# A two-layer RWKV/S5 trunk on one core: state-space tables made in whole-tensor operations, low-rank weights scaled once, and squares summed on TensorE in the last norm

## The chip, the cores and the metric

The kernel runs on one core of a Trainium2 chip. The metric is the device time of one execution in microseconds (us); lower is better. PE is TensorE, DVE VectorE, ACT ScalarE, POOL GpSimd, SP SyncE (its queue issues all DMAs of this kernel).

## The reference, cut to what matters

1024 tokens of width 1024 go through two layers in float32, each a token mixer and a squared-ReLU MLP, each followed by a LayerNorm of `alpha*x + f(x)`. What the change touches:

```
xw = x + xx * mu[1]; xa = x + xx * mu[4]; xg = x + xx * mu[5]   # xx: the token before, minus x
tanh(xw @ w1);  xa @ a1;  sigmoid(xg @ g1)                       # low-rank factors of RWKV
abar = exp(dt * lam); bbar = coef * b                            # S5, complex, 64 groups x 64 states x 16 channels
layer_norm(alpha * h + mlp(h))                                   # the last of the four norms
```

## The kernel before, in words

All activations lie transposed, 128 channels on the partitions, as eight tiles of 512 tokens for each half H of the sequence. A float32 product is three matmuls: weight and operand are split into a rounded part and the rest (`split`: an ACT cast, L151, and a DVE subtraction, L152), and `mm3` adds hi*hi, hi*lo and lo*hi; all of these are on L203. Weights come in tiles of 128x512 (256 KB) through `wraw` (2 buffers), `whi` and `wlo` (3 each). Where both halves need the same weight, the first writes the rest `wlo` to DRAM (L183) and the second loads it (L177).

- **Low-rank factors** (`rwkv_proj`, once for each half). `x + xx*mu` times a weight W is `x @ ((1-mu)W)` plus the shifted `x @ (mu W)`. `scaled` loads W, lets POOL multiply it by `1-mu` or `mu` (L330), splits it and multiplies. `shifted` calls it twice for `wa1` and twice for `g1a`; `gate_c` calls it once, with both scalings side by side. That is ten weight tiles for each half.
- **Tables of S5** (`s5_tables`, rank 99500, run beside the first half's MLP, the second half's output projection and its first norm). L1080 to L1090 make the powers 0 to 8 of 32 complex numbers on each partition, one power after the other, six DVE operations each. For each of eight f, `bc` is loaded (L1129), `bb` made in six small DVE operations (L1135 to L1140), and `ca` and `bp` expanded: two products on POOL (L1152, L1155), two on DVE (L1153, L1156), and a sum each (L1154, L1157); `ca` also gets a change of sign (L1159). Then `ca` goes to DRAM (tC, L1163), PE multiplies it with `bb` (L1170), transposes `bp` (L1186), and the results go out through `kpad` (L1179, eight DMAs of 64 KB) and `bs` (L1188). `ca`, `bp`, `bc`, `bs` have one buffer each.
- **Last norm** (`last_norm`, in two parts c of 256 tokens). TensorE makes the mean (L929), DVE subtracts it from eight tiles (L932), ACT squares them (L934, L937), six additions on DVE and POOL (L938) leave two sums, which four matmuls turn into column sums (L942). Then comes the power on POOL (L945), a spread and transposes (L947, L950), the product (L952), scale and bias (L956 on ACT, one tile on POOL), and the store.

The order on each engine and queue is static. A planner simulates the program and issues, on each engine, the ready instruction of lowest rank; the waits at run time are semaphores, and every engine and queue runs strictly in that order. MLP work has rank 200000 and more, the norms 99000, so tables come before the MLP and after a norm.

Of the kernel before, what the change touches and what calls it, by code (L numbers as in the profile page):

```python
# [8 lines left out]
F32 = mybir.dt.float32  # L9
# [49 lines left out]
MIX0R = 1500  # L59
EVB = 4  # L60
# [11 lines left out]
def trunk(ctx, tc, A):  # L72
# [120 lines left out]
    def inorder(prods):  # L193

        for x, y in zip(prods, prods[1:]):
            tc.add_manual_dep(y.ins, x.ins.name, mybir.DependencyInfo(
                mybir.DependencyClass.NoSync, mybir.DependencyReason.DATA), reason="order")

# [43 lines left out]
    def psd():  # L242
        return pd.tile([128, HT], F32, tag="d", name="d")
# [9 lines left out]
    for j in range(2):  # L253
        V.tensor_copy(pick[:, j].rearrange("p (q n) -> p q n", q=4),
                      ident[:, 64 * j : 64 * j + 32].unsqueeze(1).broadcast_to([128, 4, 32]))

    def rwkv_proj(H):
# [65 lines left out]
        def scaled(nm, parts):  # L323
            p = psd()
            n = 128 // len(parts)
            for k0 in range(0, KT, 4):
                w = first.pop(0) if first else wraw(nm, k0)
                for q, m in enumerate(parts):
                    wq = w[:, :, q * n : q * n + n]
                    G.tensor_mul(wq, wq, m[:, k0 : k0 + 4].unsqueeze(2).broadcast_to([128, 4, n]))  # L330
                hi = wp.tile([128, 4, 128], F32R, tag="whi", name="whi")
                lo = wp.tile([128, 4, 128], F32R, tag="wlo", name="wlo")
                split(w, hi, lo)
                for k in range(4):
                    mm3(p, hi[:, k], lo[:, k], xo[k0 + k][0], xo[k0 + k][1], k0 + k == 0, k0 + k == KT - 1)
            return p

        def shifted(nm, ci, js):
            p1 = scaled(nm, [mum[:, j] for j in js])
            p2 = scaled(nm, [pv[:, j] for j in js])  # L340
            e = tp.tile([128, HT], F32, tag="ev", name="e2", bufs=EVB)
            S.copy(e, p2)
            hd = tp.tile([128, HT], F32, tag="ev", name="hd", bufs=EVB)
            V.tensor_add(hd[:, 1:], p1[:, 1:], e[:, 0 : HT - 1])
            if H == 0:
                V.tensor_copy(hd[:, 0:1], p1[:, 0:1])
                V.tensor_copy(carry_p[:, ci : ci + 1], e[:, HT - 1 :])
            else:
                V.tensor_add(hd[:, 0:1], p1[:, 0:1], carry_p[:, ci : ci + 1])
            return hd  # L350
# [563 lines left out]
    def last_norm(h, gi, c):  # L914
# [15 lines left out]
        sab = tp.tile([128, 2, HW], F32, tag="la", name="sq01", bufs=2)  # L930
        for k, t in enumerate(hc):
            V.tensor_sub(t, t, pm)  # L932
            if k < 2:
                S.activation(sab[:, k], t, AF.Square)  # L934
            else:
                q = tp.tile([128, HT], F32, tag="m", name="sq")[:, 0:HW]
                S.activation(q, t, AF.Square)  # L937
                (G if k in LNT else V).tensor_add(sab[:, int(k in LNT)], sab[:, int(k in LNT)], q)  # L938
        pq = pl.tile([128, HT], F32, tag="l", name="pq")
        for t in range(2):  # L940
            for j in range(2):
                PE.matmul(pq[:, t : t + 1], sab[:, j, t * 128 : (t + 1) * 128], ones_c[:, 0:1], start=j == 0, stop=j == 1)  # L942
# [100 lines left out]
    def s5_tables():  # L1043
# [6 lines left out]
        pw = pp.tile([128, 9, 2, 32], F32, name="pw")  # L1050
# [29 lines left out]
        V.memset(pw[:, 0, 0], 1.0)  # L1080
        V.memset(pw[:, 0, 1], 0.0)
        V.tensor_mul(pw[:, 1, 0], mg, tr)
        V.tensor_mul(pw[:, 1, 1], mg, tq)
        for j in range(2, 9):
            V.tensor_mul(pw[:, j, 0], pw[:, j - 1, 0], pw[:, 1, 0])
            V.tensor_mul(sn, pw[:, j - 1, 1], pw[:, 1, 1])
            V.tensor_sub(pw[:, j, 0], pw[:, j, 0], sn)
            V.tensor_mul(pw[:, j, 1], pw[:, j - 1, 0], pw[:, 1, 1])
            V.tensor_mul(sn, pw[:, j - 1, 1], pw[:, 1, 0])
            V.tensor_add(pw[:, j, 1], pw[:, j, 1], sn)  # L1090
        for l in range(4):
            re, im = aw[:, l, :, 0], bw[:, l, :, 1]
            if l == 0:
                V.tensor_copy(re, pw[:, 8, 0])
                V.tensor_copy(im, pw[:, 8, 1])
# [15 lines left out]
        V.tensor_scalar(nr, pw[:, 1, 0], -1.0, None, op0=ALU.add)  # L1111
        ni = pw[:, 1, 1]
# [10 lines left out]
        for kpad in kpads:  # L1123
            G.memset(kpad[:, :, 0:8], 0.0)
        for f in range(KT):
            gs = slice(4 * f, 4 * f + 4)
            kpad = kpads[f % 2]
            bc = pp.tile([128, 2, 2, 4, 16], F32, tag="bc", name="bc", bufs=1)
            SP.dma_start(bc, A["s5bc"][f])  # L1129
            bb = pp.tile([128, 2, 4, 16], F32, tag="bb", name="bb", bufs=1)  # L1130
            tw = pp.tile([128, 4, 9, 16], F32, tag="tw", name="tw", bufs=1)
            w3 = tw[:, :, 0]
            sh = [128, 4, 16]
            crb, cib = cr[:, gs].unsqueeze(2).broadcast_to(sh), ci[:, gs].unsqueeze(2).broadcast_to(sh)
            V.tensor_mul(bb[:, 0], bc[:, 0, 0], crb)  # L1135
# [9 lines left out]
            def expand(out, src, npow, neg):  # L1145
                sh4 = [128, 4, npow, 16]
                pr_ = pw[:, 0:npow, 0, gs].rearrange("p j g -> p g j").unsqueeze(3).broadcast_to(sh4)
                pi_ = pw[:, 0:npow, 1, gs].rearrange("p j g -> p g j").unsqueeze(3).broadcast_to(sh4)
                sr = src[0].unsqueeze(2).broadcast_to(sh4)
                si = src[1].unsqueeze(2).broadcast_to(sh4)  # L1150
                w = tw[:, :, 0:npow]
                G.tensor_mul(out[0], pr_, sr)  # L1152
                V.tensor_mul(w, pi_, si)  # L1153
                V.tensor_sub(out[0], out[0], w)  # L1154
                G.tensor_mul(out[1], pr_, si)  # L1155
                V.tensor_mul(w, pi_, sr)  # L1156
                V.tensor_add(out[1], out[1], w)  # L1157
                if neg:
                    V.tensor_scalar(out[1], out[1], -1.0, None, op0=ALU.mult)  # L1159

            expand((ca[:, :, 0], ca[:, :, 1]), (bc[:, 1, 0], bc[:, 1, 1]), 9, True)
            expand((bp[:, :, 0], bp[:, :, 1]), (bb[:, 0], bb[:, 1]), 8, False)
# [194 lines left out]
def layout(inp):  # L1357
# [46 lines left out]
    out["s5bc"] = bc.reshape(2, 2, 128, KT, 4, 16).transpose(3, 2, 0, 1, 4, 5)  # L1404
# [17 lines left out]
```

## Time and profile before

| | us |
|---|---|
| median of 3 runs | 2694.06 (2689.92 to 2696.62) |
| the profiled execution | 2690.84 |
| its span, first to last instruction | 2689.1 |
| PE / DVE / ACT / POOL busy | 2523.7 / 1818.4 / 1147.1 / 618.4 |

The span is the sum that the views divide up; 1.7 us lie around it. Busy PE counts pipelined matmuls, so it is not PE at its peak. DVE instructions overlap by some 0.08 us, so that sums of busy times of groups are a little over the engine's own.

### The profile page before, as it was taken

To read this page: it belongs to the slowest core of one execution; us is meant where nothing else is said; L and a number is where in the kernel's file an instruction comes from. 1 tells how busy PE (TensorE), PEld (TensorE's weight loads), DVE (VectorE), ACT (ScalarE), POOL (GpSimd) and SP (SyncE) were. 2 spreads that over 40 slices of the span, in tenths; PEclk is the share of its full clock that TensorE was granted. 3 is DMA by queue.
4 is the path that set the end of the run, shared out by engine and by line. 5 is a ranking of instruction groups with operands and counts; after the bars stand their busy time and mean duration, and the time that the engine had idled before them with its cause. 6 is when DMAs were issued, how large, how long until landed. Compare 5 with 4: busy or idle time off the path is not lost.

```text
span 2689.1 us, 44215 instructions
## 1 busy us (share of the span) xinstructions
PE 2523.7 (94%) x16768; PEld 2040.7 (76%) x16768; DVE 1818.4 (68%) x3206; ACT 1147.1 (43%) x2038; POOL 618.4 (23%) x516
## 2 busy tenths in 40 slices
PE   7999979999889999999998999999989999999997
PEld 5778757788677777667876788778778887788886
DVE  7367677487896868997677553675955536855556
ACT  7555665454444333234533332445233324533334
POOL 3121552342442122342121000121210001200001
PEclk9998989998889999999999999999999999999998
DMA  4765555663322224465335432223353322333333
GB/s 150 254 206 179 162 170 169 206 184 119 96 74 91 95 91 148 134 162 150 110 114 180 134 98 96 86 90 124 95 193 99 98 95 85 122 100 94 96 96 102
DMA packets 221972, 345.92 MB, mean 129 GB/s; under 512 B 21952, under 2 KB 84544, under 8 KB 221760
## 3 DMA queue, kind: packets, MB, share of 16 engines
q1 hardware_dynamic: 221760, 343.11, 40.5%
q8 instruction: 132, 2.16, 0.3%
q14 instruction: 80, 0.66, 0.1%
HBM read 279.06 MB, written 63.96 MB: 128 GB/s over the span
## 4 chain that ended last, share of the span: by engine, by line
PE 64%; DVE 16%; DMA 9%; issue 4%; ACT 4%; POOL 2%; SPq 1%; ACTq 0%; DVEq 0%; POOLq 0%
PE d L203 56%; DVE wlo L152 3%; DMA s_y<-yg 2%; DMA wraw<-in_mw_dram 2%; DMA yl<-s_y 1%; DVE hA L1008 1%; DVE oAl L152 1%; PE pA L612 1%; ACT whi L151 1%; DMA wraw<-in_wr_dram 1%; DMA wraw<-in_wv_dram 1%; DVE hB L1008 1%; DVE qbuf L152 1%; DVE t L1238 1%; PE pbu L1226 1%
## 5 line engine op out<-in xcount | busy, mean ns | idle before, releaser
L151 ACT CAST whi<-wraw 128x512 fp32r<-128x512 f32 x668 | 413.9, 620 | 945.9 <-PE d L203 610.9
L152 DVE TENSOR_TENSOR wlo<-wraw,whi 128x512 fp32r<-128x512 f32 x668 | 501.8, 752 | 401.6 <-ACT whi L151 397.4
L203 PE MATMUL d<-qbuf,whi 128*128 128x512 f32 (+1 forms) x2112 | 656.3, 393 | 32.8 <-DVE hA L1008 15.3
L203 PEld LDWEIGHTS d<-qbuf,whi 128*128 128x128 f32 x2112 | 390.7, 191 | 130.1 <-DVE hA L1008 21.7
L203 PE MATMUL d<-qbuf,wlo 128*128 128x512 f32 (+1 forms) x1056 | 410.4, 391 | 9.2 <-DVE wlo L152 9.1
L203 PE MATMUL d<-oAh,whi 128*128 128x512 f32 (+1 forms) x960 | 385.5, 408 | 12.2 <-ACT ev L433 7.6
L992 POOL TENSOR_TENSOR rl<-rl 128x512 f32<-128x512 f32 x128 | 144.8, 1131 | 1079.8 <-ACT rl L991 1079.6
L203 PE MATMUL d<-oAl,whi 128*128 128x512 f32 (+1 forms) x960 | 381.8, 401 | 8.4 <-DVE oAl L152 8.4
L203 PE MATMUL d<-oAh,wlo 128*128 128x512 f32 (+1 forms) x960 | 382.2, 403 | 1.6 <-DMA wlo<-low 1.6
L203 PE MATMUL d<-oBh,whi 128*128 128x512 f32 x704 | 279.1, 396 | 0.0
L203 PE MATMUL d<-oBh,wlo 128*128 128x512 f32 x704 | 277.6, 395 | 1.5 <-DVE wlo L152 1.5
L203 PE MATMUL d<-oBl,whi 128*128 128x512 f32 x704 | 276.1, 392 | 0.0
L203 PEld LDWEIGHTS d<-qbuf,wlo 128*128 128x128 f32 x1056 | 201.2, 191 | 54.7 <-DVE wlo L152 13.2
L203 PEld LDWEIGHTS d<-oAh,whi 128*128 128x128 f32 (+1 forms) x960 | 183.3, 193 | 55.6 <-ACT ev L433 9.7
L203 PEld LDWEIGHTS d<-oAl,whi 128*128 128x128 f32 (+1 forms) x960 | 183.5, 193 | 47.4 <-DVE oAl L152 10.7
L203 PEld LDWEIGHTS d<-oAh,wlo 128*128 128x128 f32 (+1 forms) x960 | 183.4, 192 | 41.6 <-DMA wlo<-low 1.8
L1008 DVE TENSOR_TENSOR hB<-hB,d 128x512 f32<-128x512 f32 (+1 forms) x256 | 164.2, 650 | 60.9 <-PE d L203 58.2
L1008 DVE TENSOR_TENSOR hA<-hA,d 128x512 f32<-128x512 f32 x240 | 161.9, 682 | 53.6 <-PE d L203 51.6
L203 PEld LDWEIGHTS d<-oBh,wlo 128*128 128x128 f32 x704 | 132.6, 188 | 33.2 <-DVE wlo L152 2.1
L203 PEld LDWEIGHTS d<-oBl,whi 128*128 128x128 f32 x704 | 132.6, 188 | 29.0 <-issue 0.5
L203 PEld LDWEIGHTS d<-oBh,whi 128*128 128x128 f32 x704 | 132.6, 188 | 28.7 <-issue 1.3
L152 DVE TENSOR_TENSOR qbuf<-rl,qbuf 128x512 fp32r<-128x512 f32 x128 | 97.2, 759 | 67.7 <-ACT qbuf L151 67.3
(370 smaller groups left out, 3702.6 us busy)
## 6 DMA issues: line engine op xcount, KB each, us to landing
wraw<-in_mw_dram SPq DMA_DIRECT2D x520, 256.0 KB, 2.6
wraw<-in_glu_dram SPq DMA_DIRECT2D x64, 256.0 KB, 2.6
low<-wlo SPq DMA_DIRECT2D x52, 256.0 KB, 2.9
wlo<-low SPq DMA_DIRECT2D x52, 256.0 KB, 3.7
wraw<-in_wk_dram SPq DMA_DIRECT2D x32, 256.0 KB, 3.3
wraw<-in_wr_dram SPq DMA_DIRECT2D x32, 256.0 KB, 3.9
wraw<-in_wv_dram SPq DMA_DIRECT2D x32, 256.0 KB, 4.3
yl<-s_y SPq DMA_DIRECT2D x32, 256.0 KB, 3.1
```

The lines of the kernel that those rows point to most:

```text
L151: S.copy(hi, src)
L152: (e or V).tensor_sub(lo, src, hi.bitcast(F32))
L203: bulk.append((PE.matmul(p, w, x, **kw).ins, x.shape[-1]))
L612: prods.append(PE.matmul(pp[h][:, cc, i], D.KB[j][hs, u].rearrange("p j l -> p (j l)"), D.AR[j][hs, u].rearrange("p j l -> p (j l)"), star ...
L992: G.tensor_mul(r, r, r)
L1008: V.tensor_add(z, z, p)
L1226: PE.matmul(p[qs, g2, ri], tb[:, g2, ri, qs], u[:, 2 * g2 + par], start=True, stop=True)
L1238: e.tensor_mul(t2[:, :, ri], x[:, :, 1 - ri], bw[:, l, g0:g1, ri : ri + 1].broadcast_to([128, g1 - g0, n]))
```

## The change

1. The powers are made by doubling (1; 2; 3 and 4; 5 to 8), four DVE operations for each step, in a layout with the power innermost. `bc` is loaded whole in four DMAs, and `bb` made for all f in four DVE operations; ACT makes negated and swapped copies (`b2`, `c2`, the sign of `c1`). The expansion has no POOL operation, no change of sign, copies power 0 on ACT, and takes four DVE products and one DVE sum of both parts, for `ca` (512 and 1024 elements) and for `bp` (448 and 896).
2. `shifted` splits W unscaled and multiplies; then POOL scales the same tile by mu in place, and it is split again. The result is p(W) - p(mu W) + shifted p(mu W). The scaled pairs are written to DRAM in the first half (12 DMAs of 256 KB) and loaded in the second, without POOL, cast or subtraction. `gate_c` does the same with W and mu W side by side.
3. In the second part of the last norm TensorE adds up all eight squared tiles (16 matmuls of one column), and two tiles get scale and bias on DVE (`LNV`).

```
+    V.tensor_sub(pick[:, 0], pick[:, 0], pick[:, 1])
...
+        def scaled(nm, k0, w, parts):
+            ws = pair()
+            if (nm, k0) in low:
+                for x, kept in zip(ws, low[nm, k0]):
+                    SP.dma_start(flat(x), kept)
+                return ws
...
+                if m is not None:
+                    wq = w[:, :, q * n : q * n + n]
+                    G.tensor_mul(wq, wq, m[:, k0 : k0 + 4].unsqueeze(2).broadcast_to([128, 4, n]))
+            split(w, *ws)
...
+            for x, kept in zip(ws, low[nm, k0]):
+                SP.dma_start(kept, flat(x))
+            return ws
...
+        def shifted(nm, ci, js):
+            p1, p2 = psd(), psd()
             for k0 in range(0, KT, 4):
                 w = first.pop(0) if first else wraw(nm, k0)
+                ws = pair()
+                split(w, *ws)
+                lowmm(p1, ws, k0)
+                lowmm(p2, scaled(nm, k0, w, [pv[:, j] for j in js]), k0)
             e = tp.tile([128, HT], F32, tag="ev", name="e2", bufs=EVB)
             S.copy(e, p2)
             hd = tp.tile([128, HT], F32, tag="ev", name="hd", bufs=EVB)
-            V.tensor_add(hd[:, 1:], p1[:, 1:], e[:, 0 : HT - 1])
+            V.tensor_sub(hd, p1, e)
+            V.tensor_add(hd[:, 1:], hd[:, 1:], e[:, 0 : HT - 1])
...
+            for k0 in range(0, KT, 4):
+                w = None if ("g1c", k0) in low else wraw("g1c", k0)
+                lowmm(p, scaled("g1c", k0, w, [None, pv[:, 5]]), k0)
...
+        if c == 1:
+            sq = [tp.tile([128, 2, HW], F32, tag="ev", name="sq2", bufs=EVB) for _ in range(4)]
+            for k, t in enumerate(hc):
+                V.tensor_sub(t, t, pm)
+                S.activation(sq[k // 2][:, k % 2], t, AF.Square)
+            pq = pl.tile([128, HT], F32, tag="l", name="pq")
+            for k in range(KT):
+                for t in range(2):
+                    PE.matmul(pq[:, t : t + 1], sq[k // 2][:, k % 2, t * 128 : (t + 1) * 128], ones_c[:, 0:1],
+                              start=k == 0 and t == 0, stop=k == KT - 1, skip_group_check=True)
...
+            if c == 1 and k in LNV:
+                V.tensor_scalar(t, t, vec(g, k), vec(b, k), op0=ALU.mult, op1=ALU.add)
...
+        for j in (1, 2, 4):
+            sp_ = [128, 2, 32, j]
+            w1, w2 = (pp.tile([128, 2, 32, 4], F32, tag=nm, name=nm, bufs=1)[:, :, :, 0:j] for nm in ("wx", "wy"))
+            x, y = pw[:, :, :, 1 : j + 1], pw[:, :, :, j + 1 : 2 * j + 1]
+            V.tensor_mul(w1, x, pw[:, 0:1, :, j : j + 1].broadcast_to(sp_))
+            V.tensor_mul(w2, x, pw[:, 1:2, :, j : j + 1].broadcast_to(sp_))
+            V.tensor_sub(y[:, 0], w1[:, 0], w2[:, 1])
+            V.tensor_add(y[:, 1], w1[:, 1], w2[:, 0])
...
+        V.tensor_mul(b2, bc[:, 0], cib)
+        V.tensor_mul(bb, bc[:, 0], crb)
+        V.tensor_sub(bb[:, 0], bb[:, 0], b2[:, 1])
+        V.tensor_add(bb[:, 1], bb[:, 1], b2[:, 0])
+        S.mul(b2[:, 0], bb[:, 1], -1.0)
+        S.copy(b2[:, 1], bb[:, 0])
+        for ri in range(2):
+            S.mul(c2[:, ri], bc[:, 1, 1 - ri], -1.0)
+        c1 = bc[:, 1]
+        S.mul(c1[:, 1], c1[:, 1], -1.0)
...
+            def expand(dst, x, y, npow):
+                S.copy(dst[:, :, :, 0], x[:, :, gs].rearrange("p r g c -> p g r c"))
+                w = pp.tile([128, 4, 2, 8, 16], F32, tag="tw", name="tw", bufs=1)[:, :, :, 0 : npow - 1]
+                sh4 = [128, 4, npow - 1, 16]
+                pr_, pi_ = (pw[:, k, gs, 1:npow].unsqueeze(3).broadcast_to(sh4) for k in range(2))
+                for ri in range(2):
+                    V.tensor_mul(dst[:, :, ri, 1:], pr_, x[:, ri, gs].unsqueeze(2).broadcast_to(sh4))
+                    V.tensor_mul(w[:, :, ri], pi_, y[:, ri, gs].unsqueeze(2).broadcast_to(sh4))
+                V.tensor_add(dst[:, :, :, 1:], dst[:, :, :, 1:], w)
+
+            expand(ca, c1, c2, 9)
+            expand(bp, bb, b2, 8)
```

## Rows read from the trace of the kernel before

**Rows 1.** The page: the chain that ended last, by engine.
```profile
PE 64%; DVE 16%; DMA 9%; issue 4%; ACT 4%; POOL 2%; SPq 1%; ACTq 0%; DVEq 0%; POOLq 0%
```
**Rows 2.** Busy time by stretch: us, PE, PEld, DVE, ACT, POOL, clock, DMA share, GB/s.
```profile
1058.00:1242.00 184.00, 165.37 (x877) 125.44 (x877) 177.38 (x335) 70.59 (x122) 65.50 (x48) 0.94 0.53 148
1500.00:1720.00 220.00, 218.53 (x956) 179.32 (x956) 111.42 (x171) 69.49 (x119) 21.86 (x23) 1.00 0.31 96
```
**Rows 3.** The same stretches, L203 alone: us, PE, PEld, clock, DMA share, GB/s.
```profile
1058.00:1242.00 184.00, 143.40 (x551) 106.17 (x551) 0.94 0.53 148
1500.00:1720.00 220.00, 218.24 (x954) 178.94 (x954) 1.00 0.31 96
```
**Rows 4.** The stretch 1091 to 1242, L1170 and then L1186 alone; columns as before.
```profile
1091.00:1242.00 151.00, 17.16 (x256) 11.25 (x256) 0.95 0.55 148
...
1091.00:1242.00 151.00, 10.07 (x56) 6.91 (x56) 0.95 0.55 148
```
**Rows 5.** Waits of PE, 1058 to 1242: us in total, times, longest us.
```profile
PE d L203 <- DVE hA L1008: 7.6, 6, 2.7
...
PE pb L1186 <- DVE bp L1154: 1.4, 1, 1.4
```
**Rows 6.** Groups of DVE, 1058 to 1242: busy us, mean ns | idle before.
```profile
L1156 DVE TENSOR_TENSOR tw<-pw,bc 128x576 f32<-128x576 f32 x8 | 8.8, 1098 | 0.1
...
L1135 DVE TENSOR_TENSOR bb<-bc,q 128x64 f32<-128x64 f32 x8 | 4.9, 612 | 0.0
...
L1159 DVE TENSOR_SCALAR ca<-ca 128x576 f32<-128x576 f32 x8 | 4.7, 590 | 0.1
...
L1089 DVE TENSOR_TENSOR q<-pw 128x32 f32<-128x32 f32 x7 | 2.4, 336 | 0.1
...
L1137 DVE TENSOR_TENSOR bb<-bb,tw 128x64 f32<-128x64 f32 x8 | 1.7, 215 | 0.0
...
L1090 DVE TENSOR_TENSOR pw<-pw,q 128x32 f32<-128x32 f32 x7 | 1.2, 173 | 0.0
```
**Rows 7.** Lines L1153 and L1135: duration ns min/median/max, first and last start us.
```profile
L1153 DVE TENSOR_TENSOR tw<-pw,bb x8: 675/681/1595, 1099.2 to 1234.9; 128x512 f32<-128x512 f32 x8
...
L1135 DVE TENSOR_TENSOR bb<-bc,q x8: 206/216/1319, 1065.5 to 1217.8; 128x64 f32<-128x64 f32 x8
```
**Rows 8.** Timeline of DVE, then of POOL, at 1121 us: start, us.
```profile
1121.74 1.25 DVE L1136 TENSOR_TENSOR tw<-bc,q 128x64 f32<-128x64 f32 x1
...
1121.23 1.68 POOL L1152 TENSOR_TENSOR ca<-pw,bc 128x576 f32<-128x576 f32 x1
```
**Rows 9.** Groups of POOL, 1058 to 1242: busy us, mean ns | idle, releasers.
```profile
L1152 POOL TENSOR_TENSOR ca<-pw,bc 128x576 f32<-128x576 f32 x8 | 11.2, 1400 | 30.7 <-DMA tC<-ca 15.7 <-DVE bb L1135 7.7 <-DVE bp L1157 3.7
L1152 POOL TENSOR_TENSOR bp<-pw,bb 128x512 f32<-128x512 f32 x8 | 10.7, 1344 | 17.4 <-PE pb L1186 10.3 <-DVE ca L1157 5.2 <-DVE bb L1137 1.6
```
**Rows 10.** DMA issues: KB each, median us to landing.
```profile
tC<-ca SPq DMA_DIRECT2D x8, 512.0 KB, 4.3
```
**Rows 11.** Timeline of ACT at the start of the program.
```profile
7.04 0.62 ACT L151 CAST whi<-wsc 128x512 fp32r<-128x512 f32 x1 [1.62 <-POOL wsc L330]
```
**Rows 12.** The stretch 255 to 320, all (columns as rows 2); then `wsc` alone: DVE, ACT, POOL.
```profile
255.00:320.00 65.00, 61.66 (x683) 49.05 (x679) 47.36 (x116) 36.50 (x71) 31.60 (x31) 1.00 0.51 166
...
255.00:320.00 65.00, 7.04 (x10) 6.20 (x10) 12.54 (x16) 1.00 0.51 166
```
**Rows 13.** Timeline of the last norm: squares, column sums of both parts, last pass.
```profile
2672.71 0.72 ACT L934 ACTIVATE sq<-hB 128x256 f32<-128x256 f32 x2 [1.79 <-DVE hB L932]
...
2662.45 0.95 PE L942 MATMUL pq<-ones_c,sq 128*128 128x1 f32 x8
...
2677.54 1.86 PE L942 MATMUL pq<-ones_c,sq 128*128 128x1 f32 x8 [5.45 <-DVE sq L938]
...
2682.06 3.55 ACT L956 ACTIVATE hB<-hB,pv 128x256 f32<-128x256 f32 x7 [1.24 <-DVE hB L952]
```
**Rows 14.** Busy time by stretch at the end, columns as rows 2.
```profile
2676.00:2680.00 4.00, 1.86 (x8) 1.78 (x8) 1.17 (x3) 0.66 (x2) 0.90 (x2) 0.50 0.00 0
```

More of the change, by code (lines that the diff above doesn't have):

```diff
@@ L59 @@
 MIX0R = 1500
+LNV = (2, 5)
 EVB = 4
@@ L191, in inorder @@
                 mybir.DependencyClass.NoSync, mybir.DependencyReason.DATA), reason="order")
[L193 to L197, printed above, removed]
     bulk, hops = [], []
@@ L321, in rwkv_proj, with pair, flat, lowmm @@
                 xm = list(mixes(2))
-        def scaled(nm, parts):
-            p = psd()
-            n = 128 // len(parts)
+        def pair():
+            return (wp.tile([128, 4, 128], F32R, tag="whi", name="whi"),
+                    wp.tile([128, 4, 128], F32R, tag="wlo", name="wlo"))
+        def flat(t):
+            return t.bitcast(F32).rearrange("p k n -> p (k n)")
+        def scaled(nm, k0, w, parts):
[4 more added lines that the diff above has]
+                return ws
+            n = 128 // len(parts)
+            for q, m in enumerate(parts):
+                if m is not None:
+                    wq = w[:, :, q * n : q * n + n]
+                    G.tensor_mul(wq, wq, m[:, k0 : k0 + 4].unsqueeze(2).broadcast_to([128, 4, n]))
+            split(w, *ws)
+            low[nm, k0] = [dr.tile([128, 512], F32, name=f"sc{j}{nm}{k0}") for j in range(2)]
+            for x, kept in zip(ws, low[nm, k0]):
+                SP.dma_start(kept, flat(x))
+            return ws
+        def lowmm(p, ws, k0):
+            for k in range(4):
+                mm3(p, ws[0][:, k], ws[1][:, k], xo[k0 + k][0], xo[k0 + k][1], k0 + k == 0, k0 + k == KT - 1)
+        def shifted(nm, ci, js):
+            p1, p2 = psd(), psd()
             for k0 in range(0, KT, 4):
                 w = first.pop(0) if first else wraw(nm, k0)
[L328 to L340, printed above, removed]
+                ws = pair()
+                split(w, *ws)
+                lowmm(p1, ws, k0)
+                lowmm(p2, scaled(nm, k0, w, [pv[:, j] for j in js]), k0)
             e = tp.tile([128, HT], F32, tag="ev", name="e2", bufs=EVB)
@@ L929, in last_norm @@
             PE.matmul(pm, ones_c, x, start=k == 0, stop=k == 3)
[L930 to L942, printed above, removed]
+        if c == 1:
[8 more added lines that the diff above has]
+                              start=k == 0 and t == 0, stop=k == KT - 1, skip_group_check=True)
+        else:
+            sab = tp.tile([128, 2, HW], F32, tag="la", name="sq01", bufs=2)
+            for k, t in enumerate(hc):
+                V.tensor_sub(t, t, pm)
+                if k < 2:
+                    S.activation(sab[:, k], t, AF.Square)
+                else:
+                    q = tp.tile([128, HT], F32, tag="m", name="sq")[:, 0:HW]
+                    S.activation(q, t, AF.Square)
+                    (G if k in LNT else V).tensor_add(sab[:, int(k in LNT)], sab[:, int(k in LNT)], q)
+            pq = pl.tile([128, HT], F32, tag="l", name="pq")
+            for t in range(2):
+                for j in range(2):
+                    PE.matmul(pq[:, t : t + 1], sab[:, j, t * 128 : (t + 1) * 128], ones_c[:, 0:1], start=j == 0, stop=j == 1)
         rs = tp.tile([128, 4], F32, tag="rs", name="rs")[:, 0:2]
@@ L1048, in t32 @@
             return pp.tile([128, 32], F32, name=f"q{n[0]}")
-        pw = pp.tile([128, 9, 2, 32], F32, name="pw")
+        pw = pp.tile([128, 2, 32, 9], F32, name="pw")
         dt, lr, li, mg, th, sn, cs, tq, tr = (t32() for _ in range(9))
@@ L1079, in s5_tables @@
         V.tensor_scalar(tr, tr, -2.0, 1.0, op0=ALU.mult, op1=ALU.add)
[L1080 to L1090, printed above, removed]
+        V.memset(pw[:, 0, :, 0], 1.0)
+        V.memset(pw[:, 1, :, 0], 0.0)
+        V.tensor_mul(pw[:, 0, :, 1], mg, tr)
+        V.tensor_mul(pw[:, 1, :, 1], mg, tq)
+        for j in (1, 2, 4):
[6 more added lines that the diff above has]
+            V.tensor_add(y[:, 1], w1[:, 1], w2[:, 0])
         for l in range(4):
@@ L1093, in s5_tables @@
             if l == 0:
-                V.tensor_copy(re, pw[:, 8, 0])
-                V.tensor_copy(im, pw[:, 8, 1])
+                V.tensor_copy(re, pw[:, 0, :, 8])
+                V.tensor_copy(im, pw[:, 1, :, 8])
             else:
@@ L1110, in s5_tables @@
         V.reciprocal(den, den)
-        V.tensor_scalar(nr, pw[:, 1, 0], -1.0, None, op0=ALU.add)
-        ni = pw[:, 1, 1]
+        V.tensor_scalar(nr, pw[:, 0, :, 1], -1.0, None, op0=ALU.add)
+        ni = pw[:, 1, :, 1]
         V.tensor_mul(cr, nr, lr)
@@ L1124, in s5_tables @@
             G.memset(kpad[:, :, 0:8], 0.0)
+        bc = pp.tile([128, 2, 2, 32, 16], F32, name="bc")
+        for j in range(2):
+            for ri in range(2):
+                SP.dma_start(bc[:, j, ri], A["s5bc"][:, j, ri])
+        bb, b2, c2 = (pp.tile([128, 2, 32, 16], F32, name=nm) for nm in ("bb", "b2", "c2"))
+        sh = [128, 2, 32, 16]
+        crb, cib = (x.unsqueeze(1).unsqueeze(3).broadcast_to(sh) for x in (cr, ci))
+        V.tensor_mul(b2, bc[:, 0], cib)
[8 more added lines that the diff above has]
+        S.mul(c1[:, 1], c1[:, 1], -1.0)
         for f in range(KT):
@@ L1127, in s5_tables @@
             kpad = kpads[f % 2]
[L1128 to L1135, printed above, removed]
@@ L1161, in s5_tables @@
-            expand((ca[:, :, 0], ca[:, :, 1]), (bc[:, 1, 0], bc[:, 1, 1]), 9, True)
-            expand((bp[:, :, 0], bp[:, :, 1]), (bb[:, 0], bb[:, 1]), 8, False)
+            def expand(dst, x, y, npow):
[3 more added lines that the diff above has]
+                pr_, pi_ = (pw[:, k, gs, 1:npow].unsqueeze(3).broadcast_to(sh4) for k in range(2))
+                for ri in range(2):
+                    V.tensor_mul(dst[:, :, ri, 1:], pr_, x[:, ri, gs].unsqueeze(2).broadcast_to(sh4))
+                    V.tensor_mul(w[:, :, ri], pi_, y[:, ri, gs].unsqueeze(2).broadcast_to(sh4))
+                V.tensor_add(dst[:, :, :, 1:], dst[:, :, :, 1:], w)
@@ L1403, in layout @@
                    np.stack([states(g["s5_c_re"][0].transpose(0, 2, 1)), states(g["s5_c_im"][0].transpose(0, 2, 1))])])
-    out["s5bc"] = bc.reshape(2, 2, 128, KT, 4, 16).transpose(3, 2, 0, 1, 4, 5)
+    out["s5bc"] = bc.transpose(2, 0, 1, 3, 4)
     return {n: np.ascontiguousarray(a) for n, a in out.items()}
```

29 lines of the change are left out of this document (4 added, 25 removed).

## The prediction

> **What bounds the kernel now.** I read the chain of waits by engine first: matmuls hold 64% of it, DVE 16% [rows 1]. So only stretches where TensorE stands still can give time back. The busy time by stretch shows the one that the tables occupy: from 1058 to 1242 us DVE is busy for 177.38 of 184 us, against 111.42 of 220 in a stretch of MLP alone [rows 2]. In that MLP stretch 954 matmuls of L203 fill 220 us, 0.231 us each; in the table stretch only 551 ran [rows 3], which is 127.1 us of work. The tables' own work on TensorE is 17.16 + 10.07 us [rows 4], so TensorE had 154.3 us of work and lost 29.7. Its waits show to whom: four lines, all ended by DVE, from 7.6 down to 1.4 us, sum up to 15.1 [rows 5]. There DVE is the bound, TensorE close behind.
>
> **The tables.** DVE's table groups before [rows 6]: nine of the expansion (L1153 to L1159, first 8.8, last 4.7 us) are 61.8 us; six of `bb` (L1135 to L1140, 4.9 to 1.7) 20.8; six of the powers (L1085 to L1090, 2.4 to 1.2) 11.4. Together 94.0 us.
>
> After: an undisturbed product takes 0.206 us for 64 elements and 0.675 for 512 [rows 7], so 0.139 us and 1.047 ns for each element. That gives 0.608 us for 448, 1.077 for 896, 1.211 for 1024. For each f, `ca` is 4 x 0.675 + 1.211 = 3.91 and `bp` 4 x 0.608 + 1.077 = 3.51; eight f are 59.4 us. `bb` for all f is 2 x 1.211 + 2 x 0.675 = 3.8. The powers are six products of 64, 128 and 256 elements (1.77 us) and six sums of 32, 64 and 128 (1.30), together 3.1. Sum 66.3 us: **DVE gets 27.7 us back**, although it takes over the 32 products of POOL. The reason stands in the timeline: a product of 64 elements took 1.25 us, 1.04 over its undisturbed time, while POOL ran one of 1.68 [rows 8].
>
> The Trainium skill (SBUF — State Buffer, the part on which sides contend) says that DVE with two SBUF inputs and GpSimd share a pair of ports that one instruction holds to its end. By that rule each of 32 products at 1.37 us (mean of the two groups in [rows 9]) could stop DVE in full, 43.9 us, and the stretch would become TensorE's own; that is rival B. Rows 8 agree in kind, at 1.04 of 1.68 us.
>
> ACT takes over 16 copies of 128 elements and five of 512. At no more than the 0.62 us of its cast of 512 [rows 11] that is under 13.1 us, on an engine that was busy 70.59 of 184 us [rows 2]. I cost it at nothing; without that cover it is the casts of weights that come late. The loads of `bc` become four early ones instead of eight in the loop: nothing, and the queue of SP is the better for it.
>
> One wait moves. POOL stood 15.7 us, in three places, until tC had left `ca`, and 10.3 us until TensorE had read `bp` [rows 9]. Now DVE and ACT write these first and wait themselves; behind them stand the evictions and splits of the MLP, for which TensorE waits. tC lands 4.3 us after its issue [rows 10], and `bp`'s 3.51 us lie between, so 0.8 us stay open, 5.6 for seven f; I take half, 3, as MLP work fills part. So I take **-15.1 + 3 = -12 us**: of the 29.7 lost, what is named as DVE's. Bounds: -29.7, when TensorE loses nothing more; +10.9, when all 26.0 us of moved waits land on DVE and ACT, less 15.1.
>
> **The low-rank factors.** First half: the first weight was cast at 7.04, after ACT had stood 1.62 us for POOL's scaling [rows 11]. Unscaled weights come first now: -1.6 us. The same tiles are split afterwards, so casts and subtractions stay ten; two loads fewer for each of `wa1` and `g1a`, 12 stores more in SP's queue, each behind a split, with later loads behind it. I cost them at nothing, since the next load waits for that split anyway (it frees the buffer); a store that holds `whi` too long costs one landing, 4.3 us as for the larger tC [rows 10]. Second half: ten tiles cost DVE 7.04, ACT 6.20, POOL 12.54 us [rows 12]; six of the ten subtractions and casts go, and all of POOL's. But TensorE was busy 61.66 of 65 us there [rows 12], so I take 0. Bounds: -4.2 (six tenths of DVE's part), and +4.3 for one load of a kept pair that lands late, since 16 loads take the place of ten and each waits in SP's queue for TensorE to free its buffer, with the recurrence's loads behind. `shifted` gains one DVE operation of 512, 0.675 us, four times in all, beside matmuls. Term: **-1.6**, bounds -5.8 and +7.0.
>
> **The last norm.** Before, TensorE's column sums start at 2677.54 and end at 2679.40 [rows 13]. After, the first square is there at 2672.71 + 0.41 (an estimate from two in 0.72), 2673.1, and TensorE works behind ACT. Four matmuls were eight records: 0.95 us in the first part, 1.86 in the second [rows 13], where the granted clock was 0.50, so 1.2 GHz [rows 14], after TensorE had idled 5.45 us. Sixteen matmuls are 32 records: 3.8 us at 2.4 GHz, 7.4 at 1.2. TensorE no longer idles, so I take the first: end at 2676.9, -2.5. At the other clock it ends at 2680.5, +1.1. ACT's last pass loses two of seven tiles, 0.51 us each [rows 13]; it follows DVE, which gets them, so I take -0.4 of a possible -1.0. Term: **-2.9**, bounds -3.5 and +1.1.
>
> **Sum.** The profiled execution took 2690.84 us, its span 2689.1. -12 - 1.6 - 2.9 = -16.5 makes 2674.3. The median of the runs is 3.2 us higher, so the forecast for a median is 2677.5. About 0.3%, 8.1 us, is what a measurement of this kernel can tell from no change.
>
> **The rivals** (times as medians). A pace decides between them. Let the eight expansions occupy DVE for X us, now 151. TensorE then does 27.2 us of table work, and MLP work for what DVE has left: (X - 66.3) / 0.51, with 111.42 of 220 as DVE's need [rows 2]. X of 107 or more: nothing is lost. X = 88: 18 lost, 12 fewer than today, my forecast. X = 76: 29.7 lost, no gain. X = 66.3: 39 lost.
>
> A, the forecast, X near 88: 0.45. For it: rows 5 and 6.
>
> B, the port pair's rule in full, DVE free enough to mix: 2694.1 - 29.7 - 4.5 = 2660. For it: the stretched operations. Against: table work outranks the MLP. 0.15.
>
> C, the tables merely end sooner, X near 76: 2694.1 - 4.5 = 2689.6, no change. For it: without POOL, DVE's table operations are ready one after another. 0.22.
>
> D, slower: the same burst in full. `ca`, `bp` and the next `ca` follow each other on DVE, evictions L1008 wait behind them, TensorE loses 39 in place of 29.7: 2694.1 + 9.3 - 4.5 = 2699, and up to 2703 with the waits for tC added. It decides from X below 76, so from less than 9.5 us for one f. Against: the wait for tC and the eight small DMAs of each f keep the loop apart. 0.10.
>
> E, the last norm doesn't speed up, because TensorE's clock is halved under its one-column matmuls: 2677.5 + 2.5 + 1.1 = 2681. Against: it works from 2673.1 on without a pause. 0.08.
>
> **How the numbers follow.** A's own range, with the bounds of the low-rank part and half of the span between the ends of the tables, is 2664 to 2691. The range of 8 in 10 goes from 2656 (all of B, with the lower bounds of the rest) to 2693: below it a tenth at most is left, above it D and a late part of C. Faster by over 0.3%, below 2686: B, nearly all of A, most of E less A's tail, 0.63. Within: C and A's upper end, 0.25. Slower: D with a little of C, 0.12.
>
> **What the profile would show.** The table stretch should have DVE's table groups near 66 us, products of 512 at 0.68 and few over 1.0, and no POOL operation of the tables; L203's matmuls per us should rise over 551 in 184. If they don't, while DVE's sum has fallen, C or D holds, and the waits for DVE hA are longer than 7.6. If ACT's `ca` copies stand before tC, the moved wait is real. At the start the first cast should be near 5.4; in the last norm the column sums should end near 2.5 us earlier against the mean (L929), with the clock at 1.00. Wrong would be: no fall of TensorE's waits for DVE, or a stretch of weights waiting for DMAs that the denser tables delay.

## The result, and the profile after

The changed kernel takes 2701.98 us, the kernel before 2694.50 beside it (median of 19 runs each): ratio 1.0030, 95% interval 1.0019 to 1.0041. It is slower by about the 0.3% that the prediction took as the least that can be told from no change, and the interval is clear of 1; forecast was 2677.5. The profiled execution has a span of 2698.4 us.

The table stretch did get better. Busy time of `after` by stretch (columns as [rows 2]), then L198 alone, which was L203 (as [rows 3]):

```profile
1058.00:1242.00 184.00, 169.69 (x931) 133.00 (x929) 152.29 (x251) 77.51 (x143) 25.91 (x17) 0.97 0.57 153
...
1058.00:1242.00 184.00, 148.91 (x597) 111.89 (x595) 0.97 0.57 153
```

DVE is busy 25.1 us less than in [rows 2], POOL 39.6, and TensorE does 46 matmuls more than in [rows 3]: at 0.231 us, 10.6 us of MLP. DVE's expansion groups (as [rows 6]), the waits for tC and TensorE's two longest waits there (as [rows 5]):

```profile
L1191 DVE TENSOR_TENSOR tw<-pw,c 128x512 f32<-128x512 f32 x16 | 11.4, 754 | 0.0
L1190 DVE TENSOR_TENSOR bp<-pw,bb 128x448 f32<-128x448 f32 x16 | 10.4, 687 | 0.0
L1190 DVE TENSOR_TENSOR ca<-pw,bc 128x512 f32<-128x512 f32 x16 | 10.3, 685 | 2.0 <-DMA tC<-ca 2.0
L1191 DVE TENSOR_TENSOR tw<-pw,b 128x448 f32<-128x448 f32 x16 | 10.2, 674 | 0.0
L1192 DVE TENSOR_TENSOR ca<-ca,tw 128x1024 f32<-128x1024 f32 x8 | 9.8, 1223 | 0.1
L1192 DVE TENSOR_TENSOR bp<-bp,tw 128x896 f32<-128x896 f32 x8 | 8.7, 1087 | 0.1
...
ACT ca L1185 <- DMA tC<-ca: 4.1, 3, 2.0
DVE ca L1190 <- DMA tC<-ca: 2.0, 2, 1.1
...
PE d L198 <- DVE hA L1039: 5.9, 7, 2.0
PE d L198 <- ACT whi L152: 5.7, 2, 5.3
```

The six groups sum to 60.8 us, 59.4 was worked out; the moved wait is 6.1 us. TensorE's waits for DVE fell to 8.1 us in all, but it now waits 6.3 us for ACT, for which it had not waited there before. The start came as forecast too:

```profile
5.38 0.60 ACT L152 CAST whi<-wsc 128x512 fp32r<-128x512 f32 x1
```

So the loss lies elsewhere. I counted the matmuls on `d` of the big products (9338 in each kernel) in the order of their start, from 0. The 1000th starts at 278.7 us before and 278.5 after, the 1800th at 592.4 and 621.0, the 3400th at 1122.4 and 1148.3, the 3800th at 1255.9 and 1260.8, the last at 2667.1 and 2672.3. A lag of 19 to 29 us arises in the RWKV stage, after 280 us, where the second half's projection runs; the table stretch makes up 21 of the 26 us before it.

The last norm takes 2.1 us longer: from the end of the mean to the end of ACT's last pass 13.5 us before (2672.08 to 2685.61), now 15.7 (2678.31 to 2693.99). Its timeline (start, us), and the clock in the mean and at the sums (columns as [rows 14]):

```profile
2678.42 2.82 DVE L951 TENSOR_TENSOR hB<-hB,pm 128x256 f32<-128x256 f32 x8 [2.95 <-PE pm L946]
2678.88 2.81 ACT L952 ACTIVATE sq<-hB 128x256 f32<-128x256 f32 x8 [2.80 <-DVE hB L951]
2681.39 6.96 PE L956 MATMUL pq<-ones_c,sq 128*128 128x1 f32 x32 [3.07 <-ACT sq L952]
...
2676.00:2678.00 2.00, 2.00 (x6) 1.32 (x4) 0.00 (x0) 0.08 (x1) 0.00 (x0) 0.51 0.77 259
...
2684.00:2688.00 4.00, 4.00 (x21) 4.00 (x20) 0.00 (x0) 0.00 (x0) 0.00 (x0) 0.50 0.00 0
```

The sums don't work behind ACT. They start 0.15 us after DVE's last subtraction (2681.24): `pq` and the mean `pm` come from the PSUM pool `pl`, which has one buffer, so `pq` gets it only when all eight subtractions have read `pm`. They run at a granted clock of 0.50, to which it had fallen during the mean already, before the wait for the buffer.

### The profile page after: what moved, and what is told of

It reads as the page before. It is cut to its first block, busy times and chain, and to the rows that moved or that the text cites. A ratio compares the mean times of both kernels' runs of the same rounds, so it can differ in the third digit from the quotient of the medians.

```text
span 2698.4 us, 44100 instructions
## 1 busy us (share of the span) xinstructions
PE 2530.3 (94%) x16792; PEld 2050.4 (76%) x16792; DVE 1791.4 (66%) x3135; ACT 1150.3 (43%) x2051; POOL 556.9 (21%) x458
## 4 chain that ended last, share of the span: by engine, by line
PE 51%; DVE 10%; DMA 4%; issue 2%; ACT 2%; POOL 0%; SPq 0%; DVEq 0%; ACTq 0%; POOLq 0%
PE d L198 47%; DVE wlo L153 2%; DMA wraw<-in_mw_dram 2%; DMA s_y<-yg 1%; DVE hA L1039 1%; DMA yl<-s_y 1%; DVE t L1271 1%; DVE hB L1039 1%; PE pbu L1259 1%; PE pu L1247 1%; ACT whi L152 1%; DVE qbuf L153 1%; DVE sq L910 1%; DMA wraw<-in_wo_dram 0%; DVE tw L1191 0%
## 5 line engine op out<-in xcount | busy, mean ns | idle before, releaser
L198 PE MATMUL d<-qbuf,whi 128*128 128x512 f32 (+1 forms) x2112 | 655.7, 393 | 31.0 <-DVE hA L1039 15.6
L198 PEld LDWEIGHTS d<-qbuf,whi 128*128 128x128 f32 x2112 | 390.8, 191 | 127.5 <-DVE hA L1039 21.9
L198 PE MATMUL d<-qbuf,wlo 128*128 128x512 f32 (+1 forms) x1056 | 409.9, 391 | 8.3 <-DVE wlo L153 8.2
L198 PE MATMUL d<-oAh,whi 128*128 128x512 f32 (+1 forms) x960 | 390.7, 411 | 19.0 <-ACT ev L450 9.2
L198 PE MATMUL d<-oAl,whi 128*128 128x512 f32 (+1 forms) x960 | 385.0, 403 | 5.5 <-DVE oAl L153 5.5
L198 PE MATMUL d<-oAh,wlo 128*128 128x512 f32 (+1 forms) x960 | 385.9, 405 | 0.0
L198 PE MATMUL d<-oBh,wlo 128*128 128x512 f32 x704 | 277.2, 394 | 1.5 <-DVE wlo L153 1.5
L198 PE MATMUL d<-oBh,whi 128*128 128x512 f32 x704 | 278.3, 395 | 0.0
L198 PE MATMUL d<-oBl,whi 128*128 128x512 f32 x704 | 275.1, 391 | 0.0
L198 PEld LDWEIGHTS d<-qbuf,wlo 128*128 128x128 f32 x1056 | 201.0, 191 | 53.3 <-DVE wlo L153 12.1
L198 PEld LDWEIGHTS d<-oAh,whi 128*128 128x128 f32 (+1 forms) x960 | 186.1, 195 | 64.5 <-ACT ev L450 11.4
L198 PEld LDWEIGHTS d<-oAl,whi 128*128 128x128 f32 (+1 forms) x960 | 186.3, 195 | 44.4 <-DVE oAl L153 6.7
L198 PEld LDWEIGHTS d<-oAh,wlo 128*128 128x128 f32 (+1 forms) x960 | 185.6, 194 | 41.5 <-issue 1.3
L198 PEld LDWEIGHTS d<-oBh,wlo 128*128 128x128 f32 x704 | 132.2, 188 | 33.2 <-DVE wlo L153 2.6
L198 PEld LDWEIGHTS d<-oBl,whi 128*128 128x128 f32 x704 | 132.2, 188 | 28.9 <-issue 0.2
L198 PEld LDWEIGHTS d<-oBh,whi 128*128 128x128 f32 x704 | 132.3, 188 | 28.6 <-ACT whi L152 0.8
```

The costliest lines, as they stand in the source:

```text
L198: bulk.append((PE.matmul(p, w, x, **kw).ins, x.shape[-1]))
```

## The experiments

All times are medians beside runs of the kernel before on the same chip; ratios carry 95% intervals.

**The three parts, each alone.** Theory P: the lag of the low-rank part is a cost of its own and the tables give more than they show; rival Q: the table stretch only makes up a lag that it would make up anyway.

Tables alone (the hunks from `pw` on, and the layout of `s5bc`):

> Only part 1, the tables. Up to them the order of every engine is that of the kernel before. Theory P (costs add up: the low-rank part loses some 25 us in the RWKV stage, the tables give 22 back, the norm loses 4): 2672 to 2676, so 19 to 23 us faster, all of it gained between 1040 and 1260 us. Rival Q (in the whole change the table stretch only made up a lag that it would have made up anyway): 0 to 8 us faster. The blind prediction's term was 12 us.

Measured 2682.88 against 2693.71, ratio 0.9956 (0.9939 to 0.9972): 12 us faster, between P and Q, which asked for 19 or more and for 8 or less.

Low-rank stage alone (the hunks of `pick` and `rwkv_proj`):

> Only part 2, the low-rank factors. Theory P: the second half's projection ends late as in the whole change, some 25 us behind at 1050 us, and nothing gives it back: 20 to 26 us slower. Rival Q: the lag of 25 us at 1050 us shrinks to under 8 in the old table stretch: 0 to 8 us slower. Either way the loss starts after 280 us, none of it in the first 280.

Measured 2700.86, ratio 1.0026 (1.0009 to 1.0042). In its trace the 1800th matmul starts at 611.2 us, 18.9 late, the 3800th 8.5: the old table stretch makes up lag too, 11.6 us of the 20.1 at the 3400th. With 7 us slower Q holds.

Last norm alone, then with the sums in another PSUM pool:

> Only part 3, the last norm; everything up to the last norm's second part stands in the order of before. Theory P: the column sums start only when the last subtraction has read the mean, since the sums' PSUM tile is the mean's (one buffer), and run 32 records. At the half clock that is some 7 us, so from the end of the mean to the end of the sums 10 us in place of 7.3: 2 to 4 us slower. Rival (the 4 us in the whole change were the clock's phase in the mean alone): 0 to 3 us faster.

> Part 3 with the sums in another PSUM pool (two free buffers). Theory P: the first sums start 0.5 us after the first square, over 2 us earlier against the end of the mean than with the shared buffer; if the clock stays full the sums end 5 us after the mean's end (2 us faster than before), if it halves, 8 us after it (within 1 us of before). Rival (it isn't the shared buffer that holds the first sum back): start and time as with the shared buffer.

```
-            pq = pl.tile([128, HT], F32, tag="l", name="pq")
+            pq = pa.tile([128, HT], F32, tag="a", name="pq")
```

Measured 2693.85, ratio 0.9997 (0.9980 to 1.0013), and 2693.31, ratio 0.9993 (0.9973 to 1.0012). The column sums, first with `pl`, then with `pa`:

```profile
2674.10 2.73 ACT L930 ACTIVATE sq<-hB 128x256 f32<-128x256 f32 x8 [2.60 <-DVE hB L929]
2676.53 6.96 PE L934 MATMUL pq<-ones_c,sq 128*128 128x1 f32 x32 [2.99 <-ACT sq L930]
```

```profile
2676.68 2.73 ACT L930 ACTIVATE sq<-hB 128x256 f32<-128x256 f32 x8 [1.73 <-DVE hB L929]
2677.15 5.11 PE L934 MATMUL pq<-ones_c,sq 128*128 128x1 f32 x32 [1.03 <-ACT sq L930]
...
2678.00:2680.00 2.00, 2.00 (x17) 2.00 (x17) 0.96 (x3) 1.41 (x5) 0.00 (x0) 0.81 0.00 0
```

With its own buffer the sum starts 0.47 us after the first square, not 2.43, and the clock falls only while it runs, though TensorE is busy without a pause then (2.00 of 2.00 us at 0.81, after 0.97 in the 2 us before). From the end of the mean to the end of ACT's last pass that is 11.8 us against 15.6: some 2 us by the earlier start, the rest by the clock, which with `pl` was at its lower level from 2671.65 us on. That the shared buffer holds the sums back is shown; the 2 to 4 us are too small for the medians.

The parts sum to 0.2% faster, the whole is 0.3% slower.

**What in the low-rank stage costs: the form or the keeping?** Theory L: the kept tiles' loads; rival O: the new order of the whole stage.

```
             split(w, *ws)
-            low[nm, k0] = [dr.tile([128, 512], F32, name=f"sc{j}{nm}{k0}") for j in range(2)]
-            for x, kept in zip(ws, low[nm, k0]):
-                SP.dma_start(kept, flat(x))
             return ws
```

> Only the new form of the low-rank stage: factors unscaled and scaled by mu, p1 - e + e shifted, but nothing is kept: the second half loads, splits and scales again. Theory L (the kept tiles cost the time: their loads stand on SP's queue until a weight buffer is free, with later weights behind them): no lag of the projection in the second half, unit 4 of the recurrence starts within 4 us of the kernel before, 0 to 4 us faster. Theory O (the order of the whole RWKV stage shifts as soon as the first part has less work, and the new order is the worse one): unit 4 is 5 us or more late here too, and the time is 3 to 9 us longer.

Measured 2692.10, ratio 0.9994 (0.9979 to 1.0008). Unit 4 of the recurrence, the first of the second half (609.0 us before), starts 2.4 us late, the 3000th matmul 7.1 early: theory L's forecast. The 1800th is 9.8 us late, so not all of the lag read there in the changed kernel is the keeping's. The other way round, the old form with all ten scaled pairs kept:

```
+                if key in low:
+                    for x, kept in zip((hi, lo), low[key]):
+                        SP.dma_start(x.bitcast(F32).rearrange("p k n -> p (k n)"), kept)
+                else:
...
+                    for x, kept in zip((hi, lo), low[key]):
+                        SP.dma_start(kept, x.bitcast(F32).rearrange("p k n -> p (k n)"))
```

> Only the keeping: the factors scaled by 1-mu and mu as before, all ten pairs of tiles written out in the first half and loaded back in the second. 20 kept loads in the second half in place of 10 raw ones (12 in the changed kernel). Theory L: the second half's projection is late by more than in the low-rank stage alone, 6 to 15 us longer than before. Theory O: what decides is the new order, which may fall either way: within 9 us of before on either side, with the SP queue's wait for weight buffers no predictor of it.

Measured 2715.53, ratio 1.0085 (1.0065 to 1.0104), unit 4 22 us late. No tile kept, twelve, twenty: -2, +7, +23 us (the twenty with the old form). L has the sign, and misses by asking for less; in this trace 4.7 us of the lag stand at the 400th matmul, in the first half, where no kept tile is loaded yet. That SP's queue is the reason, as L says, is a claim of its own, tested below.

**Two parts at a time.**

> Tables and low-rank stage, the last norm as before. If the parts add up: -0.44% + 0.26% = 0.18% or 5 us faster than before (2689). If the tables' gain is lost behind the lag that the low-rank stage brings to them (the whole was 0.30% slower, the three parts sum to 0.2% faster): 3 to 9 us slower than before.

> Tables, and the last norm's sums in another PSUM pool so that they start before the last subtraction; low-rank stage as before. If the parts add up: -0.44% - 0.07% = 0.5% or 14 us faster (2680). If the tables' gain of the first run was luck of that chip: 0 to 5 us faster.

Measured 2699.06, ratio 1.0015 (1.0001 to 1.0030), and 2686.48, ratio 0.9973 (0.9958 to 0.9989). The first is 4 us slower, as if the tables' gain were lost; the second 7 us faster, between its expectations. Against the low-rank stage alone (1.0026) and the norm alone (0.9993) the tables still gain 3 and 5 us, less than by themselves, but the intervals leave the second unsure.

**Stores or loads, SP's queue or not.**

```
-            if (nm, k0) in low:
-                for x, kept in zip(ws, low[nm, k0]):
-                    SP.dma_start(flat(x), kept)
-                return ws
```

The stores run in the first half only.

> The new form of the low-rank stage, and its twelve tiles written out in the first half, but never loaded: the second half loads, splits and scales again. The form alone gave 0.9994, form, stores and loads 1.0026. Theory S (the stores cost, behind which SP's queue holds later weights in the first half): 4 us or more over the form alone, about 1.002, and the lag is there before 280 us. Theory L2 (the loads cost, in the second half): within 2 us of the form alone, 0.998 to 1.000, unit 4 of the recurrence not late.

Measured 2692.99, ratio 1.0005 (0.9992 to 1.0017): the stores cost little or nothing. Next, with `S.dma_start(flat(x), kept)` in that place:

> The low-rank stage as changed, but the twelve kept loads are issued from ACT's queue instead of SP's. Theory Q (a kept load that waits for a weight buffer holds up what stands behind it in SP's queue): most of the lag goes, ratio near 0.9994. Theory B (the buffers: a kept tile holds one of three weight buffers from its issue to its last matmul, 3 to 5 us longer than a cast does, and TensorE has less ready; the queue does not matter): as with SP's queue, 1.002 to 1.004, or worse as ACT now waits itself.

Measured 2701.34, ratio 1.0032 (1.0017 to 1.0047). Q falls: without the loads in SP's queue the loss is the same. In this trace the last steps of the stage, which will matter below, come on time, the shift's matmul 2.0 us after the last product.

**The best of the parts, and half of the tables.**

> All three parts without what cost: tables, low-rank form with nothing kept, last norm with the sums in another PSUM pool. If the parts add up (tables -0.3 to -0.4%, form -0.06%, norm -0.07%): 11 to 14 us faster. If the sink near 1494 us takes what the form brings (TensorE waits there for the activation, and its clock falls): like tables and norm alone, 8 us faster.

Measured 2679.11, ratio 0.9957 (0.9941 to 0.9974): without the keeping the parts add up.

```
-                    V.tensor_mul(w[:, :, ri], pi_, y[:, ri, gs].unsqueeze(2).broadcast_to(sh4))
-                V.tensor_add(dst[:, :, :, 1:], dst[:, :, :, 1:], w)
```

> The tables alone, with half of the expansion's products and its sums left out (so the S5 tables and all that follows from them have other values; DVE is spared some 40 of 60 us, all else in the stretch is as in the tables' run). Theory D (DVE still bounds the table stretch): 10 us or more faster than the tables alone, 2672 or less. Theory M (the stretch is no longer the bound: what is won there is lost at the end of the S5 stage, where the MLP work that fills TensorE runs out): within 4 us of the tables alone, 2680 to 2688.

Measured 2684.25, ratio 0.9967 (0.9950 to 0.9984), no better than the tables whole. The stretch, tables alone and then halved:

```profile
1058.00:1242.00 184.00, 170.41 (x918) 131.79 (x917) 156.04 (x275) 82.10 (x153) 28.34 (x18) 0.96 0.62 173
```

```profile
1058.00:1242.00 184.00, 165.99 (x906) 128.36 (x905) 118.32 (x227) 80.21 (x152) 24.70 (x18) 0.97 0.59 167
```

DVE has 37.7 us less to do and TensorE does no more. After the change DVE no longer bounds the tables. M has the time, but not the way to it: at the 3800th matmul, right after the tables, the lead over the kernel before is 4.4 us, with the tables whole 4.3, so there was no further gain to lose later.

**Traffic, and the keeping taken out of the whole.** The copies stand where the kept loads stood; the other run has the first diff of this group on the whole change.

```
+            else:
+                for j, kept in enumerate(low[nm, k0]):
+                    SP.dma_start(dr.tile([128, 512], F32, name=f"sd{j}{nm}{k0}"), kept)
```

> The form with its twelve stores, and in the second half, at the places of the kept loads, twelve copies of the same tiles from DRAM to DRAM: the traffic (read and written, so twice that of the loads) without the weight buffers; weights are loaded, split and scaled again as in the form alone. Theory T (the traffic of the kept tiles slows the loads around them): 4 us or more over the stores alone (1.0005), 1.002 to 1.004. Theory B (a kept tile costs by holding a weight buffer while it is under way): within 2 us of the stores alone, 0.9995 to 1.0015.

> The whole change but for the keeping: tables, the low-rank stage's new form computed again in the second half, last norm as changed. If keeping is the one step that turns the change into a loss: 9 to 13 us faster than before (0.995 to 0.9965), 18 us or so better than the whole. If the parts clash in another way: within 0.2% of before.

Measured 2690.44, ratio 0.9985 (0.9974 to 0.9997): the traffic costs nothing that shows. T falls, and B's range is missed on the fast side: the kernel with the copies is 0.2% faster than the one with the stores alone. The order of TensorE's records differs between these two at 4550 of 16768 places; a changed order seems to be worth that much, in either direction. And 2678.70, ratio 0.9951 (0.9937 to 0.9965): **the keeping alone turns the change into a loss**, 0.79% or 21 us in the whole. The traces of these two kernels, the whole and the whole without keeping, keep the same time up to the second low-rank stage (within 4.4 us at the 1000th matmul), though their orders differ from 82 us on. TensorE at its end, with keeping:

```profile
313.60 1.56 PE L605 MATMUL pb<-rksel,kf 64*64 64x1 f32 x32 [3.08 <-POOL kf L600]
315.09 1.87 PE L568 MATMUL pss<-hsel,sq 128*128 128x2 f32 x8
316.82 2.06 PE L387 MATMUL d<-e,pick 128*128 128x512 f32 x2
318.80 1.12 PE L742 MATMUL pX<-o,XT 64*64 64x64 f32 x16
319.85 1.59 PE L388 MATMUL d<-e,pick 128*128 128x511 f32 x2
```

and without:

```profile
304.32 1.03 PE L640 MATMUL pT<-ident,KB 128*128 128x128 f32 x8
305.44 1.13 PE L384 MATMUL d<-e,pick 128*128 128x512 f32 x2
306.41 1.02 PE L385 MATMUL d<-e,pick 128*128 128x511 f32 x2
...
309.57 1.10 PE L602 MATMUL pb<-rksel,kf 64*64 64x1 f32 x32
```

Both have their first low-rank product at 268.6 and 265.1 us, the last at 309.1 and 304.1. Then the shift's matmul comes 7.7 us later with keeping, 1.3 without: the planner has put it behind the next unit's `pb` and `pss`, and `pb` waits 3.08 us for POOL. Its input, ACT's copy `e`, was there at 311.90 us, 4.9 us before. ACT too has `hd` behind the next unit's work, with a wait for a DMA, but what `hd` waits for last is TensorE:

```profile
311.32 0.58 ACT L385 COPY e<-d 128x512 f32<-128x512 f32 x1
...
316.65 0.60 ACT L588 ACTIVATE kf<-lda,kam,pv 128x256 f32<-128x256 f32 x1 [3.99 <-DMA lda<-s_a]
...
321.60 0.60 ACT L394 ACTIVATE hd<-d 128x512 f32<-128x512 f32 x1 [0.80 <-PE d L392]
```

So `rates`, the next product, begins at 321.5 us instead of 307.5.

**Is it that place in the queues?** In the second half the stage gets a priority ahead of the recurrence; the control is the same without keeping.

```
+        with rank(15000) if H else nullcontext():
-        hd = shifted("wa1", 0, (1, 4))
+            hd = shifted("wa1", 0, (1, 4))
```

> The whole change, kept tiles and all, but in the second half the low-rank stage gets a priority ahead of the recurrence's next units, so that its last steps (the copy and the two matmuls of the shift) stand ahead of the recurrence's pb and pss in TensorE's queue, as they do without keeping; in the changed kernel they stand behind these, which wait for POOL and a DMA. Theory P (the keeping costs by the place that the planner gives these steps in the queues): the loss goes, 2676 to 2690, within 6 us of its control. Theory B (a kept tile costs by holding a weight buffer while it is under way): 2697 or more, 12 us or more above the control.

> The control: the same priority, nothing kept. Its order was already so, and should hardly change: 2676 to 2684 by both theories.

Measured 2692.14, ratio 1.0001 (0.9990 to 1.0012), and 2674.56, ratio 0.9934 (0.9920 to 0.9947), the fastest version. The gap goes from 0.79% to 0.67%, no clear difference with intervals of some 0.1% to either side of each ratio; the two kernels gain 0.29 and 0.17% by the priority. When the n-th matmul starts, in us, with keeping less without:

| matmul | 1000 | 1200 | 1800 | 3000 | 3800 | last |
|---|---|---|---|---|---|---|
| the whole (e14: 274.1, 382.8, 602.2, 999.1, 1238.8, 2650.4) | +4.4 | +17.1 | +18.8 | +25.3 | +22.0 | +21.9 |
| with the priority (e16: 277.5, 381.6, 588.2, 991.2, 1231.2, 2650.0) | +3.0 | +3.6 | +13.0 | +16.5 | +15.2 | +12.7 |

The priority removes the lag where the shift was late: 13 us between the 1000th and the 1200th matmul become 0.6. That is no scatter: six kernels with the order of the kernel before, itself among them, need 115.6 to 118.5 us for this stretch. But the loss doesn't go. P asked for at most 6 us above the control, and 17.6 remain; and with the loads in ACT's queue the shift came in time and the ratio was 1.0032. So the place says where that lag arises, and not what the 21 us are.

B's gap of 12 us or more is met, B's mechanism isn't shown. With the priority the last kept load is issued at 298.4 us. The lag grows from 4.6 us at the 1550th matmul to 13.5 at the 1700th, from 531.4 to 583.0 us, while `wr` and `wv` run and no kept tile is under way. There, with keeping, TensorE waits 2.8 us for one of ACT's splits and runs at half clock from 544.0 to 561.1 us; without, it runs at half clock for 3.4 us. That stretch, with keeping and without (columns as [rows 2]):

```profile
470.00:600.00 130.00, 118.20 (x1232) 100.46 (x1231) 91.95 (x189) 67.61 (x129) 54.76 (x43) 0.92 0.59 185
...
470.00:600.00 130.00, 121.88 (x1321) 105.24 (x1319) 94.81 (x204) 68.17 (x130) 57.58 (x44) 0.97 0.67 207
```

TensorE's 16792 records stand in another order at 4306 places, nearly all between 250 and 1250 us. What the runs leave is this: keeping changes the planner's order far beyond the stage, and in these traces time is lost at several places of it. Which of them count in the median, and whether held weight buffers stand at the start, stays open; tiles of their own for the kept weights weren't tried.

## Why the prediction was wrong

**Tables, -12: the size held, in part by luck.** Alone they gave 12 us, 7 to 16 by the interval. DVE's sums and the products of 512 (685 and 754 ns) came as worked out, and the wait for tC at 6.1 us where 5.6 were worked out and 3 taken. The Trainium skill (SBUF — State Buffer, Who interferes with whom) says that a DVE instruction with two SBUF inputs contends with a GpSimd instruction that reads SBUF. The traces agree in kind: the 576-element product took 1098 ns beside POOL [rows 6], where the prediction's line gives an estimate of 742 undisturbed, and products of 512 took 685 and 754 with POOL off the tables. But -12 was made of 15.1 us of waits for DVE that should all go. 8.1 of them stayed and 6.3 for ACT came. [rows 5] were read too neatly, too: between the first and the last of their lines stands one of 3.3 us that no engine ended.

The pace that decided between A, B, C and D, (X - 66.3) / 0.51, is refuted. From the first expansion to the last DVE took 149.7 us before, 109.7 with the tables alone, 104.6 in the whole and 80.0 with half the products. By the formula 109.7 is rival B, 30 us faster, and so is 80.0, since DVE's table work is then 37.7 us under 66.3; both measured 9 to 12 faster. For the kernel before, X of 151 and 94.0 us of table work, it gives 12 us lost, and not the 29.7 that it started from: that could have been seen ahead. D's 2699 to 2703 has the measured time by luck, since the tables lost nothing.

**Low-rank factors, -1.6: the failed step.** The form gave 1.6 us (0.9994, an interval that holds 0), and the first half went as written: first cast at 5.38, stores free within the interval. The step that failed is "But TensorE was busy 61.66 of 65 us there [rows 12], so I take 0", with a bound of one late landing, 4.3 us. Keeping costs 21 us in the whole, 9 in the low-rank stage alone. A busy TensorE says only that the stretch itself loses little: from the first low-rank product to the last it is 40.5 us with keeping and 39.0 without. The runs show the loss behind the stage: 13 us of lag where the shift stands behind work that waits, and, with that place mended, 17.6 us of the median still, with a lag that comes near 550 us in waits and at half clock. No run names one cause for all of it. I counted the waits behind SP's queue, and neither the priorities nor the planner's order.

**Last norm, -2.9: wrong in sign in the trace, too small for the medians.** "TensorE works behind ACT" overlooked that `pq` and `pm` share one PSUM buffer. "TensorE no longer idles, so I take the first" chose the wrong clock: in the changed kernel it was at 0.50 before the sums began, and with a buffer of their own it fell under the sums while TensorE was busy, which fits rival E's reason. E's size was right, 6.96 us for 32 records, 7.4 forecast; with the late start the trace has +2.1, and the part alone 0.9997.

**The sum.** Tables, form and norm, 11.9 + 1.6 + 0.8 = 14.3 us by their ratios, are what the whole without keeping gives, 13.2 (16.5 forecast); each ratio carries some 4 us to either side, so the match is closer than they can vouch for. No rival had the 21 us, so the range missed.

## What to carry to other kernels

- Keeping a product instead of computing it again is no saving where the engines that compute it have time: here it spared DVE, ACT and POOL work in a stretch with room for it, and cost 21 us.
- In a planned kernel an edit changes the order of queues far from where it stands. Compare the orders of the two programs, and look for dependent steps that moved behind another chain's waiting instruction; busy times don't show them. One such move explained 13 us of lag here, and mending it alone did not win back the loss.
- A reduction that is to overlap the readers of an earlier one needs its own PSUM buffer: here it started 2 us earlier by that.

## What was not expected

Coming early doesn't always pay. At the end of the S5 stage TensorE's other work can run out: in the trace of the tables alone it waits there for the activation, and its granted clock falls:

```profile
PE d L197 <- ACT rl L985: 3.4, 1, 3.4
...
1488.00:1496.00 8.00, 4.59 (x17) 3.47 (x16) 5.13 (x8) 3.77 (x7) 1.05 (x1) 0.80 0.47 152
1496.00:1500.00 4.00, 4.00 (x11) 3.08 (x11) 2.43 (x5) 1.21 (x2) 0.00 (x0) 0.54 0.50 162
```

The kernel before, later by 4.9 us at the 4400th matmul, has its clock at 1.00 there, and at the 4600th the lead is 0.7. This profiled run took 2692.14 us, 9 more than its kernel's median, so most runs cannot have lost as much. A single trace of this kernel places a time to some 5 us to either side: among kernels with the same order up to there the 1000th matmul starts between 271.7 and 281.4 us.
